# A transformer layer on one core: two input loads and squares, three stores, one flag and two turns are moved

## The chip, the cores and the metric

The kernel runs on one core of one Trainium2 chip. The metric is the device time of one execution in microseconds (us); lower is better. Three runs of the kernel before gave 1862.23, 1863.76 and 1865.61 us, so the median is 1863.76. A core has five engines, each with its own instruction stream in order: PE (matrix products; transposes run there too), DVE (elementwise work on vectors), ACT (copies, casts, squares and functions), POOL and SP. In this kernel SP and POOL mainly issue DMAs, and ACT issues a few. [...] A DMA issued by SP is seen in the profile on queue q1, one by POOL on q0, one by ACT on q10.

## The reference

One encoder layer on 1024 rows of width 1024, all in fp32:

```python
x += 0.5 * rmsnorm(swiglu(rmsnorm(x, pre1), w_gate1, w_up1, w_down1), post1)     # FFN 1, d_ff = 2816
qkv = rmsnorm(x, mix_pre) @ w_qkv                                                # 16 heads of 64
x += rmsnorm([norm(neighbourhood(q,k,v)) | norm(dilated(q,k,v))] @ w_out, mix_post)
x += 0.5 * rmsnorm(swiglu(rmsnorm(x, pre2), w_gate2, w_up2, w_down2), post2)     # FFN 2
rmsnorm(v, g) = v * rsqrt(mean(v*v) + 1e-6) * g;   swiglu = (silu(v @ w_gate) * (v @ w_up)) @ w_down
```

## The kernel before

**Precision.** Every product is made of three matmuls: each operand is split into a high part (a cast on ACT, `whi`, `pw`, `x..`) and a low part (a subtraction on DVE, `wlo`, `pw`, `x..`), and `mm3` adds high*high, high*low and low*high (lines 371 to 373). So each weight tile of 128x1024 costs one ACT cast and one DVE subtraction before PE can use it; the third matmul of a block is the first that reads the low part.

**Seven products for eight.** The large products use a Strassen-like scheme. The row tiles 0 to 3 give the operands A11 and A12, and tiles 4 to 7 give, together with 0 to 3, A22 and the sums S1 to S4 (`Operand`). To make them a row tile is normalised, transposed on PE (`trp`, line 273, into one of two PSUM buffers), and split (lines 279 and 280). `op.put(t)`, written `U(t)` in the plans, queues these steps for tile t; a step runs after every second product of a block (`c.step`).

**Blocks and early blocks.** A `PairGemm` goes through its weight blocks twice. The early blocks (`PairGemm.ahead`) only need A11 and A12, so they run while tiles 4 to 7 are still being prepared. For each early block b: 12 matmuls with A11 into a bank, a copy `s1` of the bank on ACT (`save`, line 484) that is stored to DRAM (`s1d`), then, one block later, 12 more matmuls with A12 into the same bank, which must wait for that copy; then `sink.first`. For the gates of the FFN the sink applies Silu and stores the tile `sg` to DRAM as `sgd` (`GatePairs.first`, lines 650 to 660). In FFN 1 the first three blocks are begun in a start of their own (`begin`), with A12 in a bank of their own: there the result is added into the `s1` tile itself, Silu is applied in place, and `s1` is what line 660 stores. The `s1` tiles come from a pool of three buffers at that stage, so the copy for block 3 needs the buffer of block 0.

**What sets the order.** PE's order is written out. The other engines' instructions are ordered by a scheduler that goes by its own estimates, unless something is tied: `c.behind(f, E, ...)` issues what f issues after the last instruction so far on engines E; `queued(f)` is `behind` for SP and POOL; `op.pinned` ties the steps of a tile's norm behind DVE's last instruction. `plan(n, {turn: [...]})` gives work to turns, one turn for each block or group.

**The start of FFN 1.** Input tiles 4 and 5 are loaded by SP; tiles 6 and 7 (`L(6, 7)`, line 1596) by POOL in turn 2, and `F(6, 7)` in turn 4 takes their squares on ACT (line 196). POOL's queue also holds the stores of the normalised tiles 0 to 3 (line 1656) and their reloads (line 300).

**From the first FFN to q, k and v.** `vp` computes the values in passes (weights `pw`, line 746 cast, 747 subtraction, copies `vt` line 1787). During it `fin.rest` finishes rows 4 to 7 of the first FFN's output (line 891, then squares, then the norm, line 255): `A(4, 5)` in turn 2 and `A(6, 7)` in turn 6. Then a `PairGemm` for q and k runs eight early blocks, with the turns of tiles 4 to 7, and the passes of `vp` go on (`vp.run(2, 3)`), for which SP reloads a tile `hb` of partial values (line 1851).

Of the kernel before, what the change touches and what calls it, by code (L numbers as in the profile page):

```python
# [16 lines left out]
SP, POOL, DVE, ACT, PE = [getattr(mybir.EngineType, e) for e in ("SP", "Pool", "DVE", "Activation", "PE")]  # L17
# [624 lines left out]
class GatePairs:  # L642
# [7 lines left out]
    def first(self, b, ps, keep, s1=None):  # L650
        c, nc = self.c, self.c.nc
        sg = s1 if keep and s1 is not None else (c.sp.tile([P, T], F32, tag="s1", name="sg") if keep else self.tile())
        if s1 is not None:
            nc.vector.tensor_add(sg, ps, s1)
            ps = sg
        nc.scalar.activation(sg, ps, AF.Silu)
        self.sg[b] = sg
        if keep:
            self.sg[b] = d = c.dr.tile([P, T], F32, name="sgd")
            nc.gpsimd.dma_start(d, sg)  # L660

    def tile(self):
        return self.c.cp.tile([P, T], F32, tag="g1", name="sg", bufs=3)
# [723 lines left out]
def layer(tc, a, out):  # L1387
    nc = tc.nc
    c = Ctx(tc)
    with ExitStack() as ctx:  # L1390
# [3 lines left out]
        def sub():  # L1394
            return ctx.enter_context(ExitStack())
# [37 lines left out]
        def down_sums(w, ts):  # L1433
            return RightSums(c, [([w[g, i].rearrange("p (j x) -> p j x", j=2) for g in range(2)], ts[i])
                                 for i in range(NPAIR)]).steps()

        def value_sums(w, ts):
            return RightSums(c, [([w[g, i // 2:i // 2 + 3:2, :, i % 2 * T:i % 2 * T + T].rearrange("j p x -> p j x")
                                   for g in range(2)], ts[i]) for i in range(4)]).steps()

        def plan(n, at, flush=True):

            if flush:
                c.flush()

            def turn(fs):
                return lambda: [f() for f in fs]
            c.todo.extend(turn(at.get(i, ())) for i in range(n))

        def one_a_turn(steps, n, first, more):  # L1450
            plan(n, {i: steps[i - first:i - first + 1] * (i >= first) + more.get(i, []) for i in range(n)})
# [17 lines left out]
        def gate_pairs(which, op, wg, wu, early):  # L1469
            return PairGemm(c, op, [(wg[f], wu[f]) for f in range(NF)], early, GatePairs(c, which))  # L1470
# [103 lines left out]
        def next_head():  # L1574
            if len(loaded) < 2 + (len(heads) > 9):
                load_head()
            return loaded.popleft()

        def queued(f):

            c.behind(f, SP, POOL)


        s1, s2, xas = sub(), sub(), sub()
# [3 lines left out]
        with ExitStack() as order:  # L1588
# [4 lines left out]
            def load(ts, queues):  # L1593
                for t, q in zip(ts, queues):
                    xs[t] = c.xp.tile([P, D], F32, tag="x", name="x", bufs=4)
                    q.dma_start(xs[t], x0[t])
            xs = {}
            op0 = Operand(c, None, 0, False)

            def begin(pg):  # L1600
# [79 lines left out]
                def products(b, kinds, cols):  # L1680
                    if b == len(acc):
                        acc.append(pg.bank())
                    for kind in kinds:
                        w, x = pg.w[b][kind == 2], op0.x[A11][kind == 1]
                        for k in range(4):
                            nc.tensor.matmul(acc[b][:, cols], w[:, 0, k * P:k * P + P], x[:, k, cols],
                                             start=kind == 0 and k == 0, stop=kind == 2 and k == 3)
                first, second, every = slice(0, 256), slice(256, 512), slice(0, 512)

                for t in range(4):  # L1690
# [89 lines left out]
            F = lambda *ts: lambda: op0.norm(ts, [xs[t] for t in ts])  # L1780
            L, U = (lambda *ts: lambda: load(ts, [nc.gpsimd] * 2)), (lambda t: lambda: op0.put(t))
# [11 lines left out]
            def values_ahead(stack, op):  # L1793
# [6 lines left out]
                def load():  # L1800
# [3 lines left out]
                    for i in range(2):  # L1804
                        vp[0].load(raws.tile([P, 2, T], F32, tag="raw", name="praw"))
                return {13: [lambda: queued(load)], 20: [lambda: vp[0].fetch()]}
            op, fin, hs, prep = ffn(1, op0, prep, gate_pairs(1, op0, a["wg1"], a["wu1"], 10), get1,
                                    {0: [lambda: c.behind(two, ACT)], 2: [L(6, 7), fifth], 3: [U(4)],
                                     4: [lambda: setattr(op0, "pinned", False), F(6, 7), U(5)], 5: [U(6)], 6: [U(7)]},
                                    down_sums(a["wd1"], ts1), value_sums(a["wv"], tsv),  # L1810
                                    a["ffn1_post_g"], a["mix_pre_g"], x0, x1, begin,
                                    lambda pool, e: bias_steps(c, a["na_rel_bias"], a["t5_rel_bias"], a["onehot"],
# [8 lines left out]
            for i in range(4):  # L1821
                vts.append(c.vt.tile([P, 4 * VW], F32, tag=f"v{i}", name="vt"))
                nc.gpsimd.memset(vts[i].rearrange("p (h f) -> p h f", f=65)[:, :, 64:65], 1.0)
            U = lambda t: lambda: op.put(t)
            A = lambda *ts: lambda: fin.rest(ts, hs.get)
            pg = PairGemm(c, op, [(a["wqk"][p], a["wqk"][8 + p]) for p in QK_ORDER], 8, QKPairs(c))
            pg.raws = early[1]
            pg.place = {b: lambda: early[0]().rearrange("p h m x -> h p m x") for b in (0, 3, 6)}
            op.pinned = True
            plan(16, {0: [lambda: fin.scale(4, 4), lambda: fin.rows(range(4, 8))], 2: [A(4, 5)], 6: [A(6, 7)],  # L1830
                      9: [lambda: queued(pg.start)], 10: [U(4)],
                      11: [lambda: c.behind(lambda: pg.split_left(0), DVE, ACT)]})
            vp.run(0, 1, upto=1)
            e.close()
            early_pools(e, 2, 2)
            c.qs, c.qkbufs = c.sp, 2
            plan(8, {0: [U(5)], 2: [U(6)], 4: [U(7)]}, False)
            pg.ahead()
            c.flush()
            e.close()  # L1840
# [102 lines left out]
        with ordered(DVE, ACT):  # L1943
# [13 lines left out]
            for p in range(NP, 2 * NP):  # L1957
                for hd in range(2):
                    d, st, g = next_head()
# [38 lines left out]
        with ordered():  # L1998
# [9 lines left out]
            op = Operand(c, g3, 2)  # L2008
# [3 lines left out]
            fin = Finish(c, x1, x2, p2, op)  # L2012
            fin.rows(range(4))
            hs = [part, hs1p.tile([P, 4, D], F32, name="hs")]
            A = lambda *ts: lambda: fin.rest(ts, lambda t: hs[t // 4][:, t % 4, :])
            U = lambda t: lambda: op.put(t)
# [84 lines left out]
```

## Time and profile before

| | us |
|---|---|
| median of three runs | 1863.76 |
| the profiled execution's own time | 1866.11 |
| span of the profiled execution, first to last instruction | 1864.1 |
| PE busy | 1833.0 (98%) |
| DVE busy | 1305.6 (70%) |
| ACT busy | 811.8 (44%) |
| POOL busy | 321.3 (17%) |

The 2.0 us between the span and the execution's own time lie outside the instructions. All positions below are us from the span's start. In a timeline a row has start, duration, engine, line, operation, output and input, shapes, count, and in brackets how long the engine had been idle and what released it. SPq, POOLq and ACTq rows are the issue of a DMA, not its transfer. PEclk is the clock granted to PE, 1.00 being full speed.

### The profile page before, as it was taken

The numbers are of one execution on the slowest core, as the hardware profiler recorded it, in microseconds if no ns is written. First come the engines' busy times: TensorE is split into PE (matmuls) and PEld (weight loads), VectorE is DVE, ScalarE is ACT, GpSimd is POOL, SyncE is SP. The second block draws the span as 40 slices with busy tenths as digits, with TensorE's granted clock in tenths as the row PEclk, the third lists the DMA queues.
The fourth block names the chain that finished last, engine by engine and source line by source line (L and its number), as shares of the span: only waits on it lengthen the run. The fifth ranks groups of instructions, "written<-read, shape, count | busy, mean of one in ns | idle before, by whom it ended". The sixth has DMA issues, their size and how long they took to land.

```text
span 1864.1 us, 24893 instructions
## 1 busy us (share of the span) xinstructions
PE 1833.0 (98%) x8952; PEld 1528.9 (82%) x8952; DVE 1305.6 (70%) x2138; ACT 811.8 (44%) x1330; POOL 321.3 (17%) x519
## 2 busy tenths in 40 slices
PE   7999999999999998999999999999999999999998
PEld 6788878888888877788899988878888888888886
DVE  6788777776664967468666766777888777755557
ACT  4522233333453646323577766564222333344433
POOL 1111221222100012222343310021111111110000
PEclk9999999999999999999999999999999999999999
DMA  7645558787986756746884643485455656596564
GB/s 265 220 159 183 169 188 253 226 243 262 353 298 200 251 201 237 244 153 204 291 288 152 210 149 119 161 307 193 156 194 181 243 205 233 191 325 200 194 229 151
DMA packets 164990, 404.62 MB, mean 217 GB/s; under 512 B 18881, under 2 KB 35489, under 8 KB 162818
## 3 DMA queue, kind: packets, MB, share of 16 engines
q1 hardware_dynamic: 115664, 228.30, 37.2%
q0 software_dynamic: 48336, 172.63, 26.4%
q10 hardware_dynamic: 866, 2.10, 0.3%
q8 instruction: 70, 1.15, 0.3%
q14 instruction: 54, 0.44, 0.1%
HBM read 276.95 MB, written 131.07 MB: 219 GB/s over the span
## 4 chain that ended last, share of the span: by engine, by line
PE 91%; DMA 3%; DVE 3%; ACT 2%; issue 1%; POOL 0%; DVEq 0%; ACTq 0%; POOLq 0%
PE mmp L371 17%; PE mmp L373 17%; PE mmp L372 17%; PE accp L372 10%; PE accp L371 10%; PE accp L373 10%; PE po L1198 3%; PE ptp L1086 2%; PE sp L1186 1%; PE po L1319 1%; DMA graw<-in_wg_dram 1%; PE trp L273 1%; PE sp L1306 1%; DMA xn<-xn 1%; DMA hb<-vs 1%
## 5 line engine op out<-in xcount | busy, mean ns | idle before, releaser
L371 PE MATMUL mmp<-x,whi 128*128 128x512 f32 x1412 | 559.1, 396 | 3.8 <-ACT s L484 3.6
L373 PE MATMUL mmp<-x,wlo 128*128 128x512 f32 x1412 | 555.5, 393 | 4.3 <-DVE wlo L466 4.3
L372 PE MATMUL mmp<-x,whi 128*128 128x512 f32 x1412 | 553.9, 392 | 0.2 <-DVE x L1671 0.2
L373 PEld LDWEIGHTS mmp<-x,wlo 128*128 128x128 f32 x1412 | 265.9, 188 | 66.6 <-DVE wlo L466 6.3
L371 PEld LDWEIGHTS mmp<-x,whi 128*128 128x128 f32 x1412 | 266.0, 188 | 64.3 <-ACT s L484 3.8
L372 PEld LDWEIGHTS mmp<-x,whi 128*128 128x128 f32 x1412 | 266.0, 188 | 58.5 <-DVE x L1671 0.5
L747 DVE TENSOR_TENSOR pw<-praw,pw 128x1024 fp32r<-128x1024 f32 (+1 forms) x182 | 198.6, 1138 | 129.3 <-ACT pw L746 129.0
L465 ACT CAST whi<-wraw 128x1024 fp32r<-128x1024 f32 x126 | 132.2, 1052 | 335.1 <-PE mmp L372 280.8
L746 ACT CAST pw<-praw 128x1024 fp32r<-128x1024 f32 (+1 forms) x182 | 169.3, 984 | 210.4 <-PE accp L373 156.7
L371 PE MATMUL accp<-pw 128*128 128x512 f32 x600 | 234.2, 390 | 0.0
L373 PE MATMUL accp<-pw 128*128 128x512 f32 x600 | 233.5, 389 | 0.0
L372 PE MATMUL accp<-pw 128*128 128x512 f32 x600 | 233.4, 389 | 0.0
L466 DVE TENSOR_TENSOR wlo<-wraw,whi 128x1024 fp32r<-128x1024 f32 x126 | 154.1, 1225 | 19.9 <-ACT whi L465 19.9
L373 PEld LDWEIGHTS accp<-pw 128*128 128x128 f32 x600 | 112.6, 188 | 23.6
L372 PEld LDWEIGHTS accp<-pw 128*128 128x128 f32 x600 | 112.6, 188 | 23.2
L371 PEld LDWEIGHTS accp<-pw 128*128 128x128 f32 x600 | 112.6, 188 | 23.1
L677 POOL DMA_DIRECT2D g<-sg x44 | 24.0, 546 | 397.3 <-DVE sg L670 211.0
L484 ACT COPY s<-mmp 128x512 f32<-128x512 f32 x52 | 30.5, 587 | 122.5 <-PE mmp L373 114.2
L557 DVE TENSOR_TENSOR wraw<-wraw 128x1024 f32<-128x1024 f32 x52 | 63.4, 1219 | 0.7
L633 DVE TENSOR_TENSOR c<-mmp,u 128x512 f32<-128x512 f32 x52 | 35.7, 686 | 35.0 <-PE mmp L373 35.0
L436 DVE TENSOR_TENSOR tr<-tr 128x1024 f32<-128x1024 f32 x26 | 31.7, 1220 | 34.1 <-DMA tr<-in_wd_dram 26.8
L623 DVE TENSOR_TENSOR c<-mmp,v 128x512 f32<-128x512 f32 x52 | 35.9, 690 | 25.9 <-PE mmp L373 25.6
(310 smaller groups left out, 2793.6 us busy)
## 6 DMA issues: line engine op xcount, KB each, us to landing
praw<-g SPq DMA_DIRECT2D x70, 512.0 KB
wraw<-in_wg_dram SPq DMA_DIRECT2D x44, 512.0 KB
wraw<-in_wu_dram SPq DMA_DIRECT2D x44, 512.0 KB
tr<-in_wd_dram SPq DMA_DIRECT2D x44, 512.0 KB
g<-sg POOLq DMA_DIRECT2D x88, 256.0 KB, 4.5
ts<-tr POOLq DMA_DIRECT2D x22, 1024.0 KB, 5.1
praw<-ts SPq DMA_DIRECT2D x88, 256.0 KB
praw<-in_wd_dram SPq DMA_DIRECT2D x66, 256.0 KB
```

The source lines that it names most:

```text
L371: nc.tensor.matmul(out, ahi, bhi, start=start, stop=False, skip_group_check=go_on)
L372: nc.tensor.matmul(out, ahi, blo, start=False, stop=False, skip_group_check=go_on)
L373: nc.tensor.matmul(out, alo, bhi, start=False, stop=stop, skip_group_check=go_on)
L465: nc.scalar.copy(hi, raw)
L466: nc.vector.tensor_sub(lo, raw, hi.bitcast(F32))
L557: nc.vector.tensor_sub(r[:, 0:2], r[:, 1:3], r[:, 0:2])
L623: nc.vector.tensor_add(c22, d, v)
L633: nc.vector.tensor_add(c21, d, u2)
L746: nc.scalar.copy(hi, x)
L747: nc.vector.tensor_sub(lo, x, hi.bitcast(F32))
L1086: c.nc.tensor.transpose(self.tps[:, j, :], self.probs[:, j * P:(j + 1) * P], c.ident)
L1198: nc.tensor.matmul(po[0][:, un * 2 + j], u.pt[:, 2 * j + t, :], rhs, start=t == 0, stop=t == 1)
```

## The change

Four things change; no arithmetic does, and PE has the same instructions.

1. `GatePairs.first`: the store of `sg` goes to ACT's queue instead of POOL's where the block was begun at the start (`s1` is given), which is the case for blocks 0, 1 and 2 of FFN 1 alone.
2. `L(6, 7)` is wrapped in `queued`, and `F(6, 7)` in `c.behind(..., ACT)`.
3. `op.pinned = True` for the q/k operand is set in turn 6 of the plan, not ahead of it.
4. In the eight early q/k blocks tile 5 starts in turn 1 (was 0) and tile 6 in turn 3 (was 2).

```diff
         if keep:
             self.sg[b] = d = c.dr.tile([P, T], F32, name="sgd")
-            nc.gpsimd.dma_start(d, sg)
+            (nc.gpsimd if s1 is None else nc.scalar).dma_start(d, sg)
...
-                                    {0: [lambda: c.behind(two, ACT)], 2: [L(6, 7), fifth], 3: [U(4)],
-                                     4: [lambda: setattr(op0, "pinned", False), F(6, 7), U(5)], 5: [U(6)], 6: [U(7)]},
+                                    {0: [lambda: c.behind(two, ACT)], 2: [lambda: queued(L(6, 7)), fifth], 3: [U(4)],
+                                     4: [lambda: setattr(op0, "pinned", False), lambda: c.behind(F(6, 7), ACT), U(5)], 5: [U(6)], 6: [U(7)]},
...
-            op.pinned = True
-            plan(16, {0: [lambda: fin.scale(4, 4), lambda: fin.rows(range(4, 8))], 2: [A(4, 5)], 6: [A(6, 7)],
+            plan(16, {0: [lambda: fin.scale(4, 4), lambda: fin.rows(range(4, 8))], 2: [A(4, 5)],
+                      6: [lambda: setattr(op, "pinned", True), A(6, 7)],
                       9: [lambda: queued(pg.start)], 10: [U(4)],
...
-            plan(8, {0: [U(5)], 2: [U(6)], 4: [U(7)]}, False)
+            plan(8, {1: [U(5)], 3: [U(6)], 4: [U(7)]}, False)
```

What it moves on the engines, at three places. The first is ACT in the early blocks of FFN 1. `s_346` and `s_372` are the `s1` tiles of blocks 0 and 1, `s_510` is the copy for block 3, `whi` are the high parts of later blocks' weights; line 196 is a square of tile 6 or 7.

```order
 L656 ACTIVATE s_346<-s_346 128x512
 L656 ACTIVATE s_372<-s_372 128x512
-L465 CAST whi<-graw 128x1024
-L196 ACTIVATE xn,ss<-x 128x1024
+L660 DMA sgd<-s_346 128x512
+L660 DMA sgd<-s_372 128x512
 L465 CAST whi<-graw 128x1024
 L484 COPY s_510<-mmp 128x512
+L465 CAST whi<-graw 128x1024
 L656 ACTIVATE s_406<-s_406 128x512
 L279 CAST x_176<-trp 128x4x128
-L196 ACTIVATE xn,ss<-x 128x1024
```

The two stores now stand on ACT right behind their Silus, the copy `s_510` ahead of one cast, and the two squares are gone from this stretch (they come some ten rows later). On POOL the two loads of tiles 6 and 7 keep their place.

The second place is DVE while the values are computed, at the finish of rows 4 to 7 of the FFN's output: before,

```order
L891 SCALAR_TENSOR_TENSOR x_5464<-hb_3813,y_5455,x_5464 128x1024
L747 TENSOR_TENSOR pw_5495<-praw_5496,pw_5495 128x1024
L891 SCALAR_TENSOR_TENSOR x_5466<-hb_3813,y_5455,x_5466 128x1024
L153 TENSOR_SCALAR v_5530<-ss_5517 128x2
L155 RECIPROCAL y_5531<-y_5531 128x2
```

and now:

```order
L891 SCALAR_TENSOR_TENSOR x_5464<-hb_3813,y_5455,x_5464 128x1024
L891 SCALAR_TENSOR_TENSOR x_5466<-hb_3813,y_5455,x_5466 128x1024
L153 TENSOR_SCALAR v_5530<-ss_5517 128x2
L155 RECIPROCAL y_5531<-y_5531 128x2
L158 TENSOR_TENSOR e_5532<-y_5531,v_5530 128x2
L159 TENSOR_TENSOR e_5532<-e_5532,y_5531 128x2
L160 SCALAR_TENSOR_TENSOR y_5531<-e_5532,y_5531 128x2
L255 SCALAR_TENSOR_TENSOR x_5464<-x_5464,y_5531,gain_4858 128x1024
L255 SCALAR_TENSOR_TENSOR x_5466<-x_5466,y_5531,gain_4858 128x1024
L747 TENSOR_TENSOR pw_5495<-praw_5496,pw_5495 128x1024
```

The low part `pw_5495` stood between the two additions of tiles 4 and 5 (`x_5464`, `x_5466`); it now stands behind the whole norm of both. Further down on DVE, in the early q/k blocks, the low part of block 2's weights stood behind the sums of tile 5 (`s_5707`), before:

```order
L280 TENSOR_TENSOR x31_5421<-s_5590,x30_5420 128x4x128
L280 TENSOR_TENSOR x61_5423<-trp_5720,x60_5422 128x4x128
L324 TENSOR_TENSOR s_5707<-x1_5627,trp_5708 128x512
L334 TENSOR_TENSOR s_5707<-trp_5720,s_5707 128x512
L335 TENSOR_TENSOR s_5707<-s_5707,x1_5627 128x512
L336 TENSOR_TENSOR s_5707<-x1_5627,s_5707 128x512
L466 TENSOR_TENSOR wlo_5737<-graw_5600,whi_5736 128x1024
```

and now stands ahead of them (it is called `wlo_5718` there, and the sums `s_5752`):

```order
L280 TENSOR_TENSOR x31_5421<-s_5590,x30_5420 128x4x128
L466 TENSOR_TENSOR wlo_5718<-graw_5600,whi_5717 128x1024
L466 TENSOR_TENSOR pw_5740<-graw_5675,pw_5740 128x1024
L1030 TENSOR_TENSOR qk_5735<-qk_5735 128x512
L324 TENSOR_TENSOR s_5752<-x1_5627,trp_5753 128x512
```

The third place is SP after the early q/k blocks, where `hb` is reloaded from `vs` among the loads of raw weights:

```order
 L743 DMA praw<-tsv_122 128x512
 L743 DMA praw<-tsv_123 128x512
-L743 DMA praw<-in_wv_dram 128x512 x2
 L1851 DMA hb<-vs_157 128x4x520
-L743 DMA praw<-in_wv_dram 128x512 x2
+L743 DMA praw<-in_wv_dram 128x512 x4
```

The load of `hb` now stands ahead of all four loads from `in_wv`, no longer behind two of them.

## The prediction

> **What bounds the kernel now.** I read the waits of PE first, then the chain of waits, then the timelines of the places that the change touches, each with a table of windows. The page says that PE is busy 98% of the span, so anything gained must come out of PE's waits or its clock. These groups of PE's waits (total us, times, longest) lie where the change works:
>
> ```profile
> PE mmp L373 <- DVE wlo L466: 4.3, 3, 1.9
> ...
> PE mmp L371 <- ACT s L484: 3.6, 1, 3.6
> ...
> PE trp L273 <- DVE x L255: 1.9, 1, 1.9
> PE accp L372 <- DVE pw L747: 1.2, 1, 1.2
> ...
> PE mmp L373 <- DVE pw L466: 0.9, 1, 0.9
> ...
> PE trp L273 <- DVE x L280: 0.4, 1, 0.4
> ```
>
> Together 12.3 us at three places. Between them PE runs without a gap, so a shift at one place carries through to the end.
>
> The 3.6 us of line 484 are in FFN 1's early blocks, and the chain of waits says where they come from:
>
> ```profile
> 27.05 10.60 DMA xn<-xn
> ...
> 38.21 0.51 POOL x L300
> 38.73 7.71 DMA sgd<-s
> 46.52 0.59 ACT s L484
> 47.16 0.80 PE mmp L371
> ```
>
> PE waits for block 3's copy, the copy waits for the buffer of block 0's `s1`, and that tile is free when its store has landed, at 46.5. The store was issued at 38.7, since POOL had stood on the reload of a tile whose own store took 10.6 us. The stop costs more than itself. In windows (length; busy time and instructions of PE, PEld, DVE, ACT, POOL; PEclk; DMA share; GB/s):
>
> ```profile
> 43.43:47.16 3.73, 0.17 (x3) 0.00 (x1) 1.23 (x1) 1.36 (x3) 0.00 (x0) 0.87 0.47 171
> 47.16:53.17 6.01, 6.01 (x16) 4.75 (x17) 4.46 (x6) 3.61 (x8) 2.15 (x4) 0.51 0.81 270
> 44.18:66.53 22.35, 19.01 (x86) 15.24 (x86) 17.27 (x32) 12.17 (x21) 4.85 (x9) 0.85 0.57 182
> 683.45:689.02 5.57, 5.57 (x26) 4.48 (x25) 0.01 (x1) 3.84 (x7) 2.18 (x4) 1.00 0.65 253
> 718.00:720.00 2.00, 2.00 (x8) 1.58 (x7) 2.00 (x3) 1.18 (x3) 0.67 (x1) 0.65 0.94 338
> 720.00:722.00 2.00, 2.00 (x6) 1.52 (x6) 1.38 (x3) 0.59 (x1) 0.27 (x2) 0.50 1.03 381
> ```
>
> After the stop the clock is at 0.51 for 6.0 us. PE's rows tell what both cost, since one product of six matmuls stands between two transposes:
>
> ```profile
> 42.99 0.60 PE L273 MATMUL trp<-ident,s 128*128 128x128 f32 x4
> ...
> 56.84 0.60 PE L273 MATMUL trp<-ident,xn 128*128 128x128 f32 x4
> ...
> 58.67 0.60 PE L273 MATMUL trp<-ident,s 128*128 128x128 f32 x4
> ```
>
> At the full clock one such step takes 58.67-56.84 = 1.83 us. The two steps from 42.99 to 53.17 (the second window's end) took 10.18 in place of 3.66: 6.5 us lost, 3.7 by the stop and 2.8 by the clock. The fourth window shows DVE idle for 5.57 us in the values' passes, the cause of the second place.
>
> **Place 1, the stores on ACT's queue and the two squares.** The rows of ACT, and the traffic of 36 to 40 us:
>
> ```profile
> 35.85 1.15 ACT L656 ACTIVATE s<-s 128x512 f32<-128x512 f32 x2
> 42.07 1.06 ACT L196 ACTIVATE xn<-x 128x1024 f32<-128x1024 f32 x1 [4.12 <-DMA x<-in_x_dram]
> 1860.72 0.34 ACTq L870 DMA_DIRECT2D out_dram<-xl  x1
> ...
> DMA packets 442, 1.62 MB, mean 406 GB/s; under 512 B 47, under 2 KB 47, under 8 KB 441
> q0 software_dynamic: 308, 1.11, 76.5%
> q1 hardware_dynamic: 133, 0.50, 31.2%
> ...
> DMA to landing us min/median/max: 2.3/3.6/7.8
> ```
>
> The Silus of blocks 0 and 1 end at 37.0; with one issue of 0.34 to 0.4 us behind them the first store leaves ACT at 37.4, not 38.7 behind POOL's reload. Its landing isn't in this trace, since no store goes by that queue here. The last row gives the landings of `sgd` from 36 to 110 us, all issued by POOL: bounds 37.4+2.3 = 39.7 and 37.4+7.8 = 45.2. Between them: q1 moved 0.50 MB in 4 us (125 GB/s) beside a full q0; 256 KB at that rate or twice it take 2.1 or 1.05 us, and at half of it 4.2, and a landing of 2.3 in a quiet stretch holds about 1.65 besides the 0.65 that 256 KB take at 406 GB/s. I take **42.0**, the middle of 41.2 (one such rate) and 43.3 (half of it), nearer to the longest landing than to the shortest, because the DMA engines are full.
>
> [...]
>
> With a landing at 42.0 the copy runs to 42.5. Its ACT neighbours: the square of tile 6 that held ACT until 43.1 (it waited for its load) is gone from here, and the cast that stood ahead of the copy now stands behind it, 42.5 to 43.5 (1.05 as for another cast of this size, quoted at place 3). PE needs the copy at 43.43: no stop, no lowered clock. The two issues delay the cast behind the Silus by 0.8 us, hidden, because its subtraction ends at about 40.1 and PE reads it at 40.2; if that cover is missed, it costs some tenths. The loads of tiles 6 and 7 keep their place on POOL and cost nothing.
>
> PE does not get the whole 6.5. From 44.18 to 66.53, where its last wait of this stretch (0.4 for line 280) ends, DVE has 17.27 us of work (third window), and PE's transposes wait for DVE to empty their buffers. Started at 43.5 with some 0.6 of idle time (a cast behind the squares, which are two times 1.15 us on ACT, now at about 49.5) this ends at 61.4, where PE's own pace would bring it to about 66.5-0.4-6.5 = 59.6. So DVE sets it: 66.5-61.4 = **5.1** us. Bounds: landing at 39.7, DVE from 43.3 on without idle time, 5.9; landing at 45.2, PE stops for 2.3 and DVE starts 3 us later, 2.2.
>
> **Place 2, the norm of tiles 4 and 5, and the turns.** DVE's rows, a square on ACT, and one of PE's waits:
>
> ```profile
> 682.17 1.28 DVE L891 SCALAR_TENSOR_TENSOR x<-hb,y,x 128x1024 f32<-128x1024 f32 x1
> 689.02 1.23 DVE L747 TENSOR_TENSOR pw<-praw,pw 128x1024 fp32r<-128x1024 f32 x1 [5.56 <-ACT pw L746]
> 690.16 1.28 DVE L891 SCALAR_TENSOR_TENSOR x<-hb,y,x 128x1024 f32<-128x1024 f32 x1
> 691.54 1.06 ACT L196 ACTIVATE junk<-x 128x1024 bf16<-128x1024 f32 x1 [2.06 <-DVE x L891]
> 693.95 1.28 DVE L255 SCALAR_TENSOR_TENSOR x<-x,y,gain 128x1024 f32<-128x1024 f32 x1
> 696.69 2.47 DVE L891 SCALAR_TENSOR_TENSOR x<-hb,y,x 128x1024 f32<-128x1024 f32 x2
> 702.44 1.22 DVE L466 TENSOR_TENSOR pw<-graw,pw 128x1024 fp32r<-128x1024 f32 x1
> 704.36 2.48 DVE L255 SCALAR_TENSOR_TENSOR x<-x,y,gain 128x1024 f32<-128x1024 f32 x2
> 708.64 0.50 PE L373 MATMUL mmp<-x,wlo 128*128 128x512 f32 x1 [1.88 <-DVE wlo L466]
> ```
>
> Line 747's low part waited 5.56 us for its cast, and the second addition (690.16), the square and the norm (693.95) stood behind it. PE then waited for that norm at 695.4 (1.87), and in q/k waited for low parts of weights: 0.86 at 703.7, 1.88 at 708.6, 1.93 at 717.3. After the last two its clock fell to 0.65 and 0.50 for 4 us (2*0.35+2*0.50 = 1.7). In all 8.2 us.
>
> Now line 891 runs at 683.45, its square on ACT 685.2 to 686.4 (behind a copy of `vt` that waits there), the norm 1.25 us later as before (692.7 to 693.95), at 687.7 to 690.3 for both tiles. Line 747 follows, to 691.5; PE needs it at about 693.8. Tiles 6 and 7: additions to 693.9, squares to 695.05, and ACT's cast of the first q/k weights to 696.1, its low part on DVE at 697.3, before PE gets there at 700.0. Their norm (2.48) and the rest then end at 703.5, and the low part of block 1 at 704.7; PE wants it at 703.3. So **1.5** us of waiting stay, one wait; the single wait of 1.87 at 695.4 did not lower the clock (the windows from 695 to 718 show 1.00). Block 2's low part now stands ahead of tile 5's sums and is ready at 709.9, where PE reads it at 710.4. Gain 8.2-1.5 = **6.7**. Bounds: 8.2 if DVE is 1.5 us better placed, 8.2-1.5-2.9 = 3.8 if the later start of tiles 5 and 6 makes one more wait of 1.9 us with a 1 us loss of clock. That later start leaves tile 7 right behind tile 6 on one buffer; some 5.4 us of DVE's other work stand between to cover its reload.
>
> [...]
>
> **Place 3, `hb` ahead of two loads.**
>
> ```profile
> 756.46 0.38 SPq L1851 DMA_DIRECT2D hb<-vs  x1
> ...
> 766.07 1.05 ACT L746 CAST pw<-praw 128x1024 fp32r<-128x1024 f32 x1 [8.29 <-PE accp L373]
> 767.06 1.89 DVE L814 TENSOR_TENSOR hb<-accp,hb 128x512 f32<-128x512 f32 x3 [8.56 <-DMA hb<-vs]
> 768.87 1.21 DVE L747 TENSOR_TENSOR pw<-praw,pw 128x1024 fp32r<-128x1024 f32 x1
> ```
>
> `hb` (1 MB) landed at 767.06, 10.6 us after its issue behind two loads of 256 KB. Without those ahead, at the 253 to 270 GB/s of the windows above, it lands 2 us sooner, at 765.1: line 814 ends at 767.0, line 747 follows its cast at 767.1 and ends at 768.3; PE wanted it at 768.9 and waited 1.2. Gain **1.2** (0 if the order of arrival does not follow the order of issue).
>
> **The sum.** 5.1+6.7+1.2 = 13.0. The profiled execution took 1866.1 (span 1864.1), so 1853.1 by its own time. It stands 2.3 above the median of the runs; against that median, 1863.8-13.0 = **1850.8**. All low bounds give 2.2+3.8+0 = 6.0 (1857.8), all high ones 5.9+8.2+1.2 = 15.3 (1848.5).
>
> **Rivals.** First, the store on ACT's queue does not pass the backlog (it does not do what it seems to): 7.8 us to landing, as the chain shows for POOL's, PE stops at the same place for 2.3 us, place 1 gives 2.2 and the time is 1853.7 (2.2+6.7+1.2 = 10.1). For it: DMA share is near full at 36 to 40. Against: q1's 0.50 MB moved beside q0's. 0.15. Second, DVE stays the bound in q/k's early blocks: from 700 to 718 PE is held by DVE, the tile work is only moved, and two waits of about 1.8 with the lowered clock (1.7) come back in later blocks in place of the one of 1.5. Place 2 gives 8.2-5.3 = 2.9, the time is 1854.6. 0.15. Third, slower: ACT's queue delays everything behind the store. If the store on it lands only 17.5 us after its issue (54.9, where the longest transfer in the chain took 10.6), the copy, the cast behind it and line 279's casts are held, PE stops for 11.5 us instead of 3.7 and the clock loses 3: 14.5-6.5 = 8.0 lost there, against 7.9 won at the other places; from there on it is slower than before, and beyond the 0.2% below with a landing 21.5 us after the issue (1867.9). 0.03. That several low ends meet and less than 0.2% is left (place 1 near 0 and one more wait at place 2): 0.05, some 1860.5.
>
> **How the numbers follow.** Forecast 0.62, rivals 0.15, 0.15, 0.03, rest 0.05. The range: 1848.0 just under the high bounds, 1858.0 just above the low ones, which holds the first two rivals. About 0.2% (3.7 us) is what a measurement of this kernel can tell from no change; the forecast and the first two rivals all lie beyond it: faster 0.92, the same 0.05, slower 0.03.
>
> **What would show it.** Right: the copy of line 484 that follows the first two stores is done by 43.5, PE's clock stays near 1.00 from 47 to 53; PE waits near 61 for line 280 at most; no wait for line 255, and one of about 1.5 us for line 466 at q/k's begin; line 814 no longer waits past 765. Wrong: a stop of PE at 43 with a store of over 6 us, waits for line 466 in blocks 3 to 7 of q/k, a clock under 0.7 behind either, or a new wait at a place outside these three, which would mean that the scheduler moved more than I followed.

## The result, and the profile after

The change makes the kernel faster: 1853.14 us median of six runs (1851.15 to 1855.15), beside 1863.54 (1861.02 to 1865.61) for the kernel before; ratio 0.9945, 95% interval 0.9932 to 0.9957. That is 10.4 us or 0.55%, and no run of the one reaches a run of the other; 13.0 were forecast. Two later comparisons gave 0.9955 (0.9939 to 0.9972) and 0.9955 (0.9943 to 0.9968), 7.3 and 7.8 us between the medians.

The profiled execution has a span of 1849.3 us, 14.8 below the one shown of before. So the two profiles differ by more than the medians do: the change's is of the shortest of its six runs (1851.15), and before's is of an execution (1866.11) longer than all six runs of that kernel. The difference has to be read with care. PE's waits after the change (total us, times, longest), places 1 to 3 and one new line:

```profile
PE trp L273 <- DVE x L280: 1.7, 2, 1.1
PE mmp L373 <- DVE wlo L466: 1.3, 2, 0.8
PE accp L371 <- DVE hb L822: 1.1, 1, 1.1
```

The waits for line 484's copy, for line 255, for line 747 and for the first low part in q/k (line 466, `pw`) are gone. The wait for line 822 was not there before; it lies at 1812 us, far from every edit.

Place 1, the timeline of ACT and PE after the change, and two windows (length; busy time and instructions of PE, PEld, DVE, ACT, POOL; PEclk; DMA share; GB/s):

```profile
35.50 0.85 ACTq L660 DMA_DIRECT2D sgd<-s  x2
41.78 0.59 ACT L484 COPY s<-mmp 128x512 f32<-128x512 f32 x1 [4.28 <-DMA sgd<-s]
...
45.23 0.66 PE L273 MATMUL trp<-ident,s 128*128 128x128 f32 x4 [1.15 <-DVE x L280]
```

```profile
44.00:47.40 3.40, 2.25 (x14) 1.82 (x14) 3.40 (x5) 2.27 (x5) 0.55 (x1) 1.00 0.75 201
47.40:50.80 3.40, 3.40 (x20) 2.77 (x19) 3.40 (x6) 3.40 (x6) 0.55 (x1) 1.00 0.91 349
```

The first store is issued at 35.5 and has landed at 41.8, where 42.0 was forecast. PE no longer waits for the copy; DVE (line 280) holds it twice, for 1.15 us at 45 and 0.57 us at 60.7, and the clock stays at 1.00.

Place 2, DVE's rows, and the one wait that is left on PE:

```profile
676.42 2.48 DVE L891 SCALAR_TENSOR_TENSOR x<-hb,y,x 128x1024 f32<-128x1024 f32 x2
...
681.88 2.48 DVE L255 SCALAR_TENSOR_TENSOR x<-x,y,gain 128x1024 f32<-128x1024 f32 x2
684.27 1.22 DVE L747 TENSOR_TENSOR pw<-praw,pw 128x1024 fp32r<-128x1024 f32 x1
...
696.97 1.22 DVE L466 TENSOR_TENSOR wlo<-graw,whi 128x1024 fp32r<-128x1024 f32 x1
...
698.24 0.50 PE L373 MATMUL mmp<-x,wlo 128*128 128x512 f32 x1 [0.82 <-DVE wlo L466]
```

The two additions stand together, the norm follows, and line 747 comes behind it without a wait. Of five losses one is left, 0.82 us.

Place 3, SP's issue and the rows of DVE and ACT:

```profile
741.20 0.64 SPq L1851 DMA_DIRECT2D hb<-vs  x1
...
750.68 1.89 DVE L814 TENSOR_TENSOR hb<-accp,hb 128x512 f32<-128x512 f32 x3 [5.30 <-DMA hb<-vs]
...
751.95 1.06 ACT L746 CAST pw<-praw 128x1024 fp32r<-128x1024 f32 x1 [7.30 <-PE accp L373]
...
753.04 1.23 DVE L747 TENSOR_TENSOR pw<-praw,pw 128x1024 fp32r<-128x1024 f32 x1 [0.47 <-ACT pw L746]
```

`hb` now lands 1.27 us before the cast of line 746 begins; before, it landed 0.99 us after it. Line 747 waits for its cast alone, and PE for nothing.

### The profile page after: what moved, and what is told of

Same layout as the page of the kernel before. It is cut to its first block, busy times and chain, and to the rows that moved or that the text cites. A ratio compares the mean times of both kernels' runs of the same rounds, so it can differ in the third digit from the quotient of the medians.

```text
span 1849.3 us, 24890 instructions
## 1 busy us (share of the span) xinstructions
PE 1826.8 (99%) x8952; PEld 1524.9 (82%) x8952; DVE 1303.7 (70%) x2138; ACT 813.3 (44%) x1330; POOL 319.8 (17%) x516
## 3 DMA queue, kind: packets, MB, share of 16 engines
q1 hardware_dynamic: 115664, 228.30, 37.4%
q8 instruction: 70, 1.15, 0.3%
## 4 chain that ended last, share of the span: by engine, by line
PE 82%; issue 10%; DVE 3%; DMA 3%; ACT 2%; POOL 0%; DVEq 0%; ACTq 0%; POOLq 0%
PE mmp L371 17%; PE mmp L373 17%; PE mmp L372 17%; PE accp L371 7%; PE accp L373 7%; PE accp L372 7%; PE po L1198 3%; PE ptp L1086 2%; PE po L1319 2%; PE sp L1186 1%; DMA xn<-x 1%; PE trp L273 1%; PE sp L1306 1%; DMA x<-x 1%; DMA graw<-in_wg_dram 1%
## 5 line engine op out<-in xcount | busy, mean ns | idle before, releaser
L465 ACT CAST whi<-traw 128x512 fp32r<-128x512 f32 x52 | 32.3, 621 | 51.6 <-DVE traw L558 51.6
```

The costliest lines, as they stand in the source:

```text
L465: nc.scalar.copy(hi, raw)
```

## Where the time went, in every profile

PE runs the same matmuls in the same order in all these kernels, apart from the place of some transposes in q/k's early blocks, and always 8952 of them. So one can take two matmuls by their number in the order and compare how long each execution took between them. The table does this for stretches named by their position in the first profile of before. Each entry is the time of the stretch less that in the shortest of the fourteen executions (the second profile of "without 1", below). In the names, 1 is the stores on ACT's queue, 2 the two ties at tiles 6 and 7, 3 the flag, 4 the turns.

| kernel | 40-75 (place 1) | 360-500 | 660-760 (place 2) | 760-775 (place 3) | 1800-1835 | span |
|---|---|---|---|---|---|---|
| before, first | 5.99 | 0.02 | 8.34 | 1.45 | 0.00 | 1864.1 |
| before, second | 1.73 | 0.02 | 8.97 | 1.63 | 0.00 | 1860.2 |
| before, third | 1.65 | 0.43 | 9.96 | 1.15 | 0.00 | 1861.6 |
| only 2 | 0.68 | 0.34 | 8.15 | 1.75 | 0.00 | 1858.6 |
| only 3 | 1.73 | 0.47 | 2.17 | 3.71 | 0.00 | 1854.9 |
| only 4 | 1.22 | 0.02 | 6.18 | 0.00 | 0.00 | 1856.2 |
| without 1 | 0.26 | 0.43 | -0.03 | 0.00 | 0.00 | 1850.1 |
| without 1, again | 0 | 0 | 0 | 0 | 0 | 1848.2 |
| only 1 | 1.91 | 0.91 | 8.33 | 1.49 | 1.67 | 1860.8 |
| only 1, again | 3.72 | 2.63 | 11.25 | 1.63 | 4.13 | 1871.0 |
| without 2 | 3.70 | 0.02 | 0.04 | 0.00 | 1.68 | 1852.5 |
| the change | 1.09 | 0.10 | -0.03 | 0.00 | 1.43 | 1849.3 |
| the change, again | 1.22 | 2.59 | -0.01 | 0.00 | 2.04 | 1854.4 |
| the change, third | 0.99 | 4.43 | -0.01 | 0.00 | 1.83 | 1854.6 |

The stretches left out lie between -1.5 and +0.9 us, without a pattern. The second and third profile of the change are of the longest run of their sets, 1.6 and 1.8 us above the median. Three things stand out, and the experiments below are read from them. The first profile of before lost 6 us at place 1, the other two 1.7. Place 2 and place 3 are emptied by edits 3 and 4. And every profile with edit 1 loses 1.4 to 4.1 us at 1800-1835, and four of six lose 0.9 to 4.4 at 360-500, while the eight without it lose nothing at the one and at most 0.5 at the other.

## The experiments

**Each edit alone.** The question was which edit carries which term. Edit 1 alone:

```diff
-            nc.gpsimd.dma_start(d, sg)
+            (nc.gpsimd if s1 is None else nc.scalar).dma_start(d, sg)
```

> The first edit alone: the stores of blocks 0 to 2 on ACT's queue, nothing else. In the instruction order the two squares already move behind the copy of block 3, the first one right behind the cast that follows the copy. The prediction's theory (the store's late issue behind POOL's reload holds PE): the first store lands at 41.5 to 43, PE's stop of 3.7 us at 43 goes, the clock stays at 1.00 from 47 to 53, and place 1 gains 4.0 to 5.1 us, up to 1 us less than with all edits because the square of tile 6 delays a Silu and a cast of the transposes by about 1.05 us. Nothing at the values and q/k. Time 1859 (1858 to 1860). Rival (the squares that wait for their load hold ACT, and the queue is indifferent): the copy is late by the square again, place 1 gains under 2.5 us, time above 1861.

Measured: 1866.49 us median of ten runs beside 1862.69, ratio 1.0013 (1.0000 to 1.0027). So it is not faster, and rather slower. The rival's time (above 1861) holds, but not its mechanism: the copy is not late by the square. The store did land as early as in the whole change (the copy begins at 41.97), PE's stop for the copy is gone, and yet place 1 was no better than in the later profiles of before (1.91 against 1.7): PE waits 2.02 us for line 280 instead.

Edit 2 alone:

```diff
-2: [L(6, 7), fifth]
+2: [lambda: queued(L(6, 7)), fifth]
-4: [lambda: setattr(op0, "pinned", False), F(6, 7), U(5)]
+4: [lambda: setattr(op0, "pinned", False), lambda: c.behind(F(6, 7), ACT), U(5)]
```

> The second edit alone: the load of tiles 6 and 7 and their squares tied to their turns, the stores stay on POOL. In the order the two stores now stand ahead of the two loads of 512 KB on POOL, and the squares have left ACT's stretch. The prediction's theory says that POOL's reload still holds the stores, but 1 MB less stands ahead of them in the queue (2.6 us at the 406 GB/s of 36 to 40 us): landing 42.5 to 44.5, PE stops for 0 to 1 us, place 1 gains 3 to 5 us, time 1859 to 1861. Rival (only a queue of its own gets the store past the traffic): it lands at 45 or later, PE stops for over 2 us, gain under 2 us, time above 1861.5. Second rival (the loads of tiles 6 and 7 come too late): a new wait of PE for tile 6's norm between 66 and 100 us.

Measured: 1860.88, ratio 0.9988 (0.9975 to 1.0001), an interval that holds "no change" as well. At place 1 its profile is 1.0 us better than the second and third of before and 5.3 better than the first. The first store landed at 42.5, 5.0 us after its issue, and PE did not stop for the copy. The stores did not need a queue of their own, so the first rival falls; no wait of PE for tile 6 appeared.

Edit 3 alone:

```diff
-            op.pinned = True
-            plan(16, {..., 2: [A(4, 5)], 6: [A(6, 7)],
+            plan(16, {..., 2: [A(4, 5)],
+                      6: [lambda: setattr(op, "pinned", True), A(6, 7)],
```

> The third edit alone: the tie of the norms is set in turn 6. The prediction's theory: DVE no longer waits 5.56 us for line 746's cast between the two additions; the norm of tiles 4 and 5 is 6 us earlier, PE's waits of 1.87 (line 255, 695) and 0.86 (first low part in q/k) go, the one of 1.88 falls to 1 to 1.5; the one of 1.93 in block 2 stays, and with one wait less near it the clock keeps 1.00 (or loses again up to 1.7). Place 2 gains 3.0 to 5.5 us, time 1858 to 1861. Rival (DVE is full anyway and the wait only moves): the waits in q/k grow by what is won, place 2 gains under 1.5 us.

Measured: 1856.95, ratio 0.9966 (0.9952 to 0.9979). Place 2, 8.3 to 10.0 us in the three profiles of before, falls to 2.2, so this edit carries 6 to 8 us of it, more than the 3.0 to 5.5 expected. What is left there are the wait of block 2's low part, 1.95 us, and one of 0.81 at q/k's begin. At place 3 it is 2 us worse than before: PE waits 1.79 us for line 747, and from 760.9 to 764.2 its matmuls come every 0.43 us in place of 0.23.

Edit 4 alone:

```diff
-            plan(8, {0: [U(5)], 2: [U(6)], 4: [U(7)]}, False)
+            plan(8, {1: [U(5)], 3: [U(6)], 4: [U(7)]}, False)
```

> The fourth edit alone: turns of tiles 5 and 6. The norm of tiles 4 and 5 stays late: waits of 1.87 and 0.86 stay. The low part of block 2's weights stands ahead of tile 5's sums: the wait of 1.93 at 717 goes with the lowered clock (1.7); and SP's load of hb stands ahead of the weights, so place 3 gains 1.2 to 1.4. Place 2 gains 2.0 to 3.6 us, sum 3.2 to 5.0, time 1858.5 to 1860.5. Rival (the tile work is only pushed on and stalls blocks 3 to 7): place 2 gains under 1 us, with waits of over 1 us for line 466 or 280 between 718 and 745.

Measured: 1856.96, ratio 0.9965 (0.9949 to 0.9980). The waits of 1.87 and 0.86 stayed, the one at block 2 went, and so did all of place 3. The load of `hb` is issued ahead of the weights in this kernel and not in that of edit 3, so place 3 belongs to edit 4. What was expected was met at place 2 (2.2 to 3.8 by the table) and place 3 (1.2 to 1.6). Its time is 5.7 us lower, somewhat more than these two together, and below the 1858.5 to 1860.5 expected.

**The kernel before, two more profiles.** In the kernels of edits 3 and 4 the early blocks are the code of before, and their place 1 had lost only 1.2 to 1.7 us. That put the size of place 1's term in doubt.

> The kernel before once more, for a second profile. New theory (place 1 was sized from an execution that is not typical: in the profiles of the third and the fourth edit alone, whose code is the same there, PE stopped only 1.0 to 1.5 us at 44 and the clock stayed at 1.00): PE's stop at 43 to 44 is under 2 us, no half clock between 46 and 53; place 2 has its waits of 1.9, 0.9, 1.9 and 1.9 us as before. The prediction's theory: a stop of 3 to 4 us and 6 us of half clock again.

> A third profile of the kernel before. Theory: PE's stop for the copy at place 1 is 0.9 to 1.9 us without half clock, as in the second profile and in those of the third and fourth edit; place 2 costs 8 to 10 us against the whole change, more or less by 1.7 for each stretch of half clock. The prediction's theory: a stop of 3 to 4 us with 6 us of half clock, as in the first.

Measured: 1862.18 and 1863.57 us. PE's waits in the second profile of before:

```profile
PE mmp L373 <- DVE wlo L466: 4.3, 3, 1.9
...
PE trp L273 <- DVE x L255: 1.9, 1, 1.9
PE mmp L371 <- ACT s L484: 1.5, 1, 1.5
PE accp L372 <- DVE pw L747: 1.3, 1, 1.3
```

The stop for the copy is 1.5 us, not 3.6, and no half clock follows it (PE's matmuls come every 0.23 us from 44.7 to 47.8); in the third profile the stretch costs the same. Why the first execution lost more shows in POOL's rows of the second:

```profile
35.69 0.53 POOL L300 DMA_DIRECT2D x<-xn  x1 [4.36 <-DMA xn<-xn]
36.20 1.09 POOL L660 DMA_DIRECT2D sgd<-s  x2
```

Here the store is issued at 36.2, in the first execution at 38.7; from issue to landing it takes 7.5 and 7.7 us. The 2.5 us lie in the reload ahead of it, which waits for the store of a normalised tile: that store was issued 0.65 us later in the first execution and took 10.6 us to land, 8.7 here. Why it took longer stays open. Over all five profiles with this code in the early blocks (before, edit 3, edit 4) the store is issued at 36.2 to 37.1 but for that one. So the loss of 6 us at place 1 is that of the first execution, whose own time (1866.11) stood 2.3 above the median of the runs shown then. The usual loss is 1.2 to 1.7. The waits of place 2 are the same in all three.

**Edit 1 again, alone and with 3 and 4.**

> The first edit alone once more, since its median was 4 us above the one of before while its profiled run was one of its fastest. Theory: in its usual run the square of tile 6, which now stands on ACT right behind the cast after block 3's copy, waits for its load past 42 and holds the Silu and the casts of the transposes behind it, so that PE stops at 43 to 48 for 2 us or more and the clock falls. Rival: place 1 is as in its first profile (4.3 us better than before's first profile) and the loss lies in the values and q/k, in several waits with two or more stretches of half clock.

> All edits but the second: the stores on ACT's queue, the square of tile 6 on ACT right behind the cast that follows block 3's copy. [...] Rival (the squares are indifferent once the store has its own queue): as the whole change within 0.5 us at place 1, wait for line 280 under 1.3 us.

Measured: 1872.81 us for the one run of edit 1 alone, and 1855.57 for all edits but the second, ratio 0.9960 (0.9946 to 0.9974). Beside the whole change on the same chip (1854.69) that is 0.9 us more, and their runs overlap, so what edit 2 is worth in the whole is read from the profiles. ACT and PE in the second profile of edit 1 alone, and two windows:

```profile
42.17 0.59 ACT L484 COPY s<-mmp 128x512 f32<-128x512 f32 x1 [4.09 <-DMA sgd<-s]
42.66 1.05 ACT L465 CAST whi<-graw 128x1024 fp32r<-128x1024 f32 x1
43.60 1.06 ACT L196 ACTIVATE xn<-x 128x1024 f32<-128x1024 f32 x1
...
45.18 0.57 ACT L279 CAST x<-trp 128x512 fp32r<-128x512 f32 x1
...
46.53 0.66 PE L273 MATMUL trp<-ident,s 128*128 128x128 f32 x4 [2.06 <-DVE x L280]
```

```profile
44.50:47.90 3.40, 1.37 (x8) 1.25 (x9) 2.59 (x4) 3.40 (x9) 0.55 (x1) 1.00 0.86 237
47.90:51.30 3.40, 3.40 (x11) 2.73 (x11) 2.95 (x6) 2.56 (x4) 0.02 (x1) 0.50 0.80 281
```

The square of tile 6 stands between the cast and the Silu. Against the expectation it does not wait for its load; its 1.06 us alone hold the cast of the transposes, DVE's line 280 and PE, which stops for 2.06 us, and behind that the clock is at 0.50 (second window). The kernel without edit 2 shows the same wait of 2.06 and the same half clock (0.50 from 48.3 to 51.7), 3.7 us at place 1. So edit 2 repairs a wait that edit 1 brings, and the rival (the squares are indifferent) falls. The rest of this long execution lies elsewhere, 2.6 at 360-500, 4.1 at 1800-1835, and 2.3 more at place 2 than in the second profile of before, with the clock at 0.50 from 696.5 to 699.9.

**Without edit 1.** If the queue is worth nothing, edits 2, 3 and 4 do as well.

> All edits but the first: stores of blocks 0 to 2 stay on POOL, where edit 2 sets them ahead of the loads of tiles 6 and 7. New theory (the stores' queue is worth little once the loads are behind them): place 1 within 1 us of the whole change, time 1852 to 1855, ratio to before 0.993 to 0.997. The prediction's theory (ACT's queue brings place 1's gain): 3 to 5 us slower than the whole change, 1856 to 1858.

> The whole change once more, beside the others on one chip. Expected by every theory: 1851 to 1855. New theory: relative to the second profile of before the gain is 8 to 9 us at place 2, 1.4 at place 3 and at most 1.5 at place 1, and no half clock between 17 and 1845. The prediction's theory: 5 at place 1.

> All edits but the first, again, now with more rounds beside the whole change on the same chip. Theory (the first edit adds nothing once the second stands): the same as the whole change within 0.1% (2 us), 1851 to 1854. Rival (the earlier store is worth its two issues on ACT): 2 us or more slower than the whole change. Second rival (the stores on ACT cost more than they bring): 2 us or more faster.

> The whole change with more rounds, to compare with the kernel without its first edit. Expected: 1852 to 1855 and ratio 0.994 to 0.996 to before; no half clock between 17 and 1845 us.

Measured, on one chip each: without edit 1 1852.17 beside the change's 1854.55, and with more rounds 1849.99 (1848.81 to 1851.36) beside 1854.69 (1853.65 to 1856.45). The ratios to before are 0.9942 (0.9927 to 0.9957) and 0.9929 (0.9915 to 0.9942) without edit 1, against 0.9955 and 0.9955 with it. In neither pair does a run of the one reach a run of the other: leaving edit 1 out saves 2.4 and 4.7 us. The first time the new theory's 1852 to 1855 was met and the prediction's 1856 to 1858 was not; the second time the expectation of "the same within 2 us" was wrong, and its second rival right. This version beats both kernels.

At place 1 the reason shows in POOL's and ACT's rows. Without edit 1 (second profile):

```profile
36.31 1.09 POOL L660 DMA_DIRECT2D sgd<-s  x2
37.39 1.07 POOL L1596 DMA_DIRECT2D x<-in_x_dram  x2
...
41.07 0.59 ACT L484 COPY s<-mmp 128x512 f32<-128x512 f32 x1 [3.94 <-PE trp L273]
```

and with the whole change (third profile):

```profile
30.48 0.53 POOL L1596 DMA_DIRECT2D x<-in_x_dram  x1
31.33 0.53 POOL L1596 DMA_DIRECT2D x<-in_x_dram  x1 [0.31 <-DMA s1d<-s]
...
36.01 0.86 ACTq L660 DMA_DIRECT2D sgd<-s  x2
...
42.24 0.59 ACT L484 COPY s<-mmp 128x512 f32<-128x512 f32 x1 [4.23 <-DMA sgd<-s]
```

On ACT's queue the store is issued 0.3 us earlier, but it lands 6.2 us after its issue, at 42.2. On POOL's queue it lands 4.7 us after its issue, at 41.0, just ahead of the transpose that releases the copy. What differs is where the two loads of 512 KB stand. With the stores on POOL, edit 2 sets them ahead of the loads; with the stores gone from POOL, the loads keep their place at 30 us, ahead of the store; from 36 to 42 us, in the first profile of the change, the DMA share is 1.00 to 1.05, and POOL's queue moves 1.28 MB beside 0.48 on ACT's. All profiles say the same, from issue to landing of the first store (on ACT's queue to the copy that waits for it): 6.6 to 7.7 us on POOL's queue behind the loads (five profiles), 6.1 to 6.4 on ACT's queue with the loads ahead (six), 4.7 to 5.0 on POOL's queue ahead of the loads (three). So setting the loads behind is worth some 2 us of landing on the same queue, the other queue less. No kernel here has the store on ACT's queue and the loads behind it. With the loads ahead, the landing is 0.2 to 1.6 us shorter on ACT's queue.

The loss at 1800-1835 was in no theory. POOL's rows at the second store of the output, without edit 1 and with the whole change:

```profile
1790.21 0.54 POOL L893 DMA_DIRECT2D out_dram<-x  x1 [150.94 <-DVE x L891]
1791.41 0.53 POOL L893 DMA_DIRECT2D out_dram<-x  x1 [0.66 <-DVE x L891]
...
1795.10 0.53 POOL L880 DMA_DIRECT2D x<-x  x1 [1.13 <-DMA out_dram<-x]
```

```profile
1795.16 0.54 POOL L893 DMA_DIRECT2D out_dram<-x  x1 [151.00 <-DVE x L891]
1798.26 0.53 POOL L893 DMA_DIRECT2D out_dram<-x  x1 [2.56 <-DVE pw L747]
...
1804.11 0.54 POOL L880 DMA_DIRECT2D x<-x  x1 [4.72 <-DMA out_dram<-x]
```

In the six profiles with edit 1 this store waits 2.56 us, until a low part of weights behind the addition is done; in the eight without it, 0.66 us, until the addition. The store is late by that, and the reload of its tile, which also waits for the store to land, by more: it is issued 8.95 us after the first store instead of 4.89. The rows that DVE adds to it are late in turn, and PE waits 1.1 to 2.2 us for line 822. The order of instructions on POOL and DVE there is the same in both kernels. Why POOL waits for line 747 there was not shown. At 360-500 PE waits mostly for copies of line 484 (0.3 to 2.0 us at a time), which stand behind DVE's work on loads of the down weights; why those come later in four of the six profiles with edit 1, and whether edit 1 is the cause, stays open.

## Why the prediction was right, and where it was wrong

The median, 1853.14, lies inside the range of 1848.0 to 1858.0 and 2.3 above the value given; the direction was right. But the terms were not all right: place 1 and two stretches that nobody had in the sum came out worse, place 2 better. That the time still lies so near the value given is in part luck. Against the mean of the second and third profile of before, the mean of the three profiles of the change stands as follows.

| term | forecast | measured |
|---|---|---|
| place 1 | 5.1 (2.2 to 5.9) | 0.6 |
| place 2 | 6.7 (3.8 to 8.2) | 9.5 |
| place 3 | 1.2 (0 to 1.2) | 1.4 |
| 360-500 | none | -2.1 |
| 1800-1835 | none | -1.8 |
| sum | 13.0 | 7.6 |

The spans of these profiles differ by 8.1, the medians by 7 to 10. The entry for 360-500 is a mean of uneven values: the three profiles of the change have 0.1, 2.6 and 4.4 there.

- **Place 1, mis-sized.** The step that failed is "6.5 us lost, 3.7 by the stop and 2.8 by the clock". It is right for the execution it was read from: against that one the change gains 4.9 in this stretch. In four of the five profiles with that code the store leaves POOL 1.6 to 2.5 us sooner, PE stops 1.0 to 1.5 us and keeps its clock (1.00 from 41 to 53 us in the profiles of edits 3 and 4), so little is there to gain. The offset of 2.3 us between that execution and the median was carried through as a constant; it was a sign that the profile held a loss that most runs do not have.
- **The landing at 42.0** came out (41.8), by two errors that cancel. The first store left ACT at 35.5, not 37.4, since its issue did not stand behind both Silus (they run from 34.84 to 35.99, and the whole stretch came 1.0 us sooner), and it took 6.3 us, not 4.6. The move of the cast behind the copy was right. "The loads of tiles 6 and 7 keep their place on POOL and cost nothing" was wrong: with the stores on POOL and the loads behind them (without edit 1), place 1 is another 1.0 us better. DVE does set the pace there, as said: both waits of PE that are left are for line 280.
- **The first rival** (the store does not pass the backlog) is half right. In the three profiles of the change the store landed 6.2 to 6.4 us after its issue, about midway between the 4.6 assumed and the rival's 7.8, and it was in time because it left ACT at 35.5 to 36.0.
- **Place 2, mechanism right, size low.** The norm behind line 747 was the cause, and edit 3 removes most of it (6 to 8 us). The wait that stays is 0.82, not 1.5, and the sum had one stretch of half clock there, as the first two profiles of before have (from 718.6 and 713.5); the third has one from 704.7 and, by its mean clock of 0.997 beside the second's 0.998, probably another. The measured 9.5 lies above the upper bound of 8.2; even against the first profile the stretch gains 8.4, about 1 us more than the listed waits and the clock give, and that rest was not followed up. The second rival (the wait comes back in later blocks) did not happen: after 698 no wait of PE for DVE is left in q/k's early blocks.
- **The clock** was read wrongly. "the single wait of 1.87 at 695.4 did not lower the clock" and "After the last two its clock fell" are right rows, but what was taken from them, that a single wait costs no clock, is wrong: in the kernel without edit 2 one wait of 2.06 us was followed by 3.4 us at 0.50. The last section has more such rows.
- **Place 3** was right: `hb` about 2 us sooner against its neighbours, 1.2 expected, 1.4 found, and tied to edit 4.
- **What was missed:** that an edit of three stores at 37 us costs 1.8 us at 1812, and perhaps up to 4.4 at 360-500. The prediction followed the order of instructions, in which nothing changes there. It had named a new wait outside the three places as a sign of being wrong, and the wait for line 822 is one.

## What to carry to other kernels

Before a stall is put into a sum, see whether a second profile of the same kernel has it; a profile above the median of the runs holds losses that the median does not. A DMA that came late because other transfers were in front of it was helped most by putting those behind it (4.7 to 5.0 us to landing, from 6.6 to 7.7); another queue helped less (6.1 to 6.4). And two profiles should be compared over their whole length, by the number of the matmul, since an edit can cost far from its place.

## What the runs showed of the hardware

In the first profile of before the clock is at 0.50 twice between 20 and 1860 us: for 6.8 us up to 53.0 and for 3.4 us from 718.6. In the second and third profile of before, in edits 2 and 4 alone, in the second profile of edit 1 alone and without edit 2, windows of 3.40 us behind a pause of PE read 0.50 or 0.51 too. Beside that stands how long PE was idle in the 3.4 us ahead. Two such windows, and the one behind each, in the kernel of edit 4 alone:

```profile
686.60:690.00 3.40, 1.59 (x7) 0.94 (x5) 2.10 (x6) 0.97 (x3) 0.36 (x1) 1.00 0.84 336
690.00:693.40 3.40, 3.34 (x19) 2.88 (x20) 3.31 (x3) 1.23 (x3) 0.54 (x1) 1.00 0.02 5
700.30:703.70 3.40, 1.55 (x8) 0.93 (x7) 3.40 (x5) 1.13 (x3) 1.75 (x4) 1.00 0.99 386
703.70:707.10 3.40, 3.40 (x10) 2.62 (x9) 1.37 (x3) 0.00 (x0) 0.00 (x0) 0.50 0.88 294
```

and in the first profile of before, where the wait of 1.87 at 695 falls into two windows:

```profile
691.30:694.70 3.40, 2.20 (x10) 1.45 (x8) 1.72 (x7) 1.35 (x3) 0.54 (x1) 1.00 0.98 355
694.70:698.10 3.40, 2.72 (x16) 2.40 (x17) 3.14 (x4) 0.62 (x2) 0.00 (x0) 1.00 0.05 17
```

In edit 4 alone, with PE busy 1.59 of 3.4 us, the next window has its full clock; with 1.55 the next is at 0.50 and holds 10 matmuls in place of 19: 1.7 us lost. In the first profile of before the wait of 1.87 at 695 is spread over two windows, 1.20 us idle in one and 0.68 in the other, and the clock stays at 1.00; ahead of 718.6 PE was idle for 1.93 us (1.47 busy), and 0.50 followed. The other windows, by their idle time: 1.94 and 1.85 us in the second and third profile of before, 2.03 and 1.87 in the second of edit 1 alone, 1.87 in edit 2 alone (the two of 1.87 in windows of 3.50 us) and the wait of 1.79 in edit 3 alone were followed by half clock; 1.81 in edit 4 alone and two of 1.82 and 1.87 in edit 2 alone were not. So all with 1.93 or more were followed by it here, and those from 1.79 to 1.87 fell on both sides; what decides between these was not shown. A wait of 1.9 us cost 1.9 us in one place (695 in the first profile of before) and 3.6 in another (717, with the 1.7 of the half clock). That is probably part of why single runs of before lie between 1859 and 1869 us; in the first profile of the change the clock is 1.00 from 17 to 1845 us, and its mean is 0.999 in all three.
